# Recurrent branch of a hybrid block: turning the values, making the states and adding up the squares at other places

## The chip, the cores and the metric

The kernel runs on one core of a Trainium2 chip. The metric is the device time of one execution in microseconds (us). The engines are named as in the profile: PE (TensorE matmul), PEld (its weight loads), DVE (VectorE), ACT (ScalarE), POOL (GpSimd), SP (the queue that issues most transfers).

## The reference, cut to what matters

One encoder layer on 512 tokens of 1024 channels: a mixer of two branches (a gated linear recurrence, HGRN2, and a long convolution, Hyena), then a retrieval layer over 16384 experts (PEER). The change lies in the recurrence, which has 8 heads with 128 keys and 128 values, and runs over the tokens in both directions.

```python
def hgrn2_chunk_scan(q, k, logf, v):
    """S_t = diag(f_t) S_{t-1} + k_t v_t^T, o_t = S_t^T q_t, chunkwise."""
    ...
    def step(state, inp):
        qb, kb, fb, vb = inp
        b = jnp.cumsum(fb, axis=2)
        inter = jnp.einsum('nhtk,nhkv->nhtv', qb * jnp.exp(b), state)
        ...
        scores = jnp.einsum('nhtk,nhsk,nhtsk->nhts', qb, kb, decay)
        intra = jnp.einsum('nhts,nhsv->nhtv', scores, vb)
        new_state = (jnp.exp(b_last[:, :, 0, :, None]) * state
                     + jnp.einsum('nhsk,nhsv->nhkv', kb * jnp.exp(b_last - b), vb))
        return new_state, inter + intra
...
    o = o2[:B] + rev(o2[B:])
    o = rmsnorm(o, hgrn_norm_g).reshape(B, L, HGRN_WIDTH)
    y_a = jnp.einsum('blc,cd->bld', (o * jax.nn.silu(og.astype(f32))).astype(xn.dtype), w_branch_a)
```

The norm needs, for each token and head, the sum of the squares of 128 outputs. The queries, the two forget gates, the values and the output gate of each head are products of the normed input with 128 columns of the input weights.

## The kernel before, in words

Channels lie on the 128 partitions, the 512 tokens along the free dimension. The recurrence takes chunks of 128 tokens (4 of them), its scores are made from seven levels of decays (L692 is the line of their small matmuls, `quarters`), and states are carried over three chunk edges in each direction.

**Projection blocks.** A product with 128 columns of weights (`proj`, `product`) is 24 matmuls: weights and inputs are each split into a rounded upper part and a rounded rest (`split`: a cast on ACT, L94, and a subtraction on DVE, L95), and `mm3` adds up three of the four products, 16 matmuls (L103, L104) and then 8 (L106), all with fp32r operands. The result stands in one of three PSUM banks (`ps_mm`). The matmuls inside the recurrence have fp32 operands that are not rounded; a matmul with fp32 operands is shown as two instructions. They write to `ps_x`, five banks.

**One head.** Head `hd` runs `scores(hd)`, a generator that yields an estimate of its cost at each step, woven with `beside(hd, work)`, which supplies projection blocks for later heads: every 6.0 (6.4 for the last head) of cost spent, one more step of `beside` is emitted. Its four steps are a query block and an output gate block for head `hd + 1`, and two forget blocks for head `hd + 2` (or blocks of branch gates, where there are no more heads). The values block of the next head comes last. In the order of the code:

- `scores`: cumulated log forgets `Z`, decayed keys `KE` and queries `QE`, the transposes of the keys (L733) and their copies `KT` on ACT (L735). Then the decays: group (6, 0, 1, 2) of the levels, each a difference on DVE (L787, L788), an exponential on ACT (L790) and products on DVE (L769, L770), then their scores (L692); then `sigmoids(hd + 1)`; then group (3, 4, 5) with its scores. The exponentials of the second group are issued behind the sigmoids, and the sigmoids behind the last exponential of the first group and behind the inverse root (`rsqrt`, L125) of `normed(hd - 1)`.
- `beside`, step 0: the query block, then `outputs(hd - 1)` (L835, L837, L839 into `po`, and the squares `o2` on ACT, L841), then `transposed(hd)`, which turns the values `vT` (L654) and copies them to `vh` on ACT (L656).
- step 1: `normed(hd - 1)`, which adds up the squares over the partitions with a matmul by a 128x128 tile of ones (L847), takes the inverse root on ACT (L124, L125) and finishes the head on DVE (L850, L851); then the second block.
- `states`, called from `scores` after the first decays: six matmuls with `KT` and `vh` (L745), and the running states `S` on DVE (L752, L754).

The tiles come from pools with one (`w1`) or two (`w2`) buffers. All engine queues are ordered at compile time by a scheduler, which goes by the order in the code and by its own estimate of when the inputs of an instruction are there: an instruction that it takes to be late is put behind later ones of its engine. The order on the chip is then fixed.

## Time and profile before

| | |
|---|---|
| median of 3 runs | 2024.74 us (2024.29 to 2025.56) |
| profiled execution | 2028.34 us |
| its span in the trace | 2026.4 us |
| granted TensorE clock | 0.999 |
| busy: PE, PEld, DVE, ACT, POOL | 99%, 87%, 82%, 49%, 27% |
| the recurrence's stretch | about 370 to 668 us |

Start with busy times and the granted clock over the span, then the chain of work that ended last, then the waits of the recurrence. [...]

### The profile page before, as it was taken

How to read it: one execution, taken by the hardware profiler on the slowest of the kernel's cores; microseconds unless marked ns; L12 is line 12 of the kernel's file. 1: busy time of each engine (PE TensorE's matmuls, PEld its weight loads, DVE VectorE, ACT ScalarE, POOL GpSimd, SP SyncE). 2: the span in 40 equal slices, each digit the busy share in tenths (PEclk: the TensorE clock that was granted, in tenths of full speed). 3: DMA queues.
4: the chain of work that ended last, by engine and by line, in shares of the span. 5: the costliest groups of instructions: out<-in, count | busy, mean ns of one | idle time of the engine just before them, and what ended most of it. 6: DMA issues, size and time to landing. Idle time of an engine off the chain costs nothing.

```text
span 2026.4 us, 32597 instructions
## 1 busy us (share of the span) xinstructions
PE 2005.6 (99%) x12553; PEld 1772.0 (87%) x12553; DVE 1660.1 (82%) x3016; ACT 984.6 (49%) x1473; POOL 548.9 (27%) x331
## 2 busy tenths in 40 slices
PE   8999999999999999999999999999999999999998
PEld 6788888888888898889999998888888888888887
DVE  6788863889987637979999968878887899888885
ACT  6555443777785624436767643333333333333333
POOL 0000000000000000000000037676766677666660
PEclk9999999999999999999999999999999999999999
DMA  5212113222222434224767998988988898999884
GB/s 192 89 53 68 63 60 106 84 74 74 74 74 75 146 125 149 97 78 165 227 202 232 287 338 317 337 309 318 364 314 314 338 365 329 357 343 333 328 296 162
DMA packets 160410, 418.09 MB, mean 206 GB/s; under 512 B 12890, under 2 KB 66012, under 8 KB 160126
## 3 DMA queue, kind: packets, MB, share of 16 engines
q1 hardware_dynamic: 115180, 263.58, 37.0%
q0 software_dynamic: 36864, 134.23, 17.9%
q10 hardware_dynamic: 8210, 18.19, 2.6%
q8 instruction: 99, 1.62, 0.3%
q14 instruction: 57, 0.47, 0.1%
HBM read 377.94 MB, written 38.01 MB: 205 GB/s over the span
## 4 chain that ended last, share of the span: by engine, by line
PE 91%; DVE 3%; issue 2%; DMA 2%; POOL 1%; ACT 1%; DVEq 0%; ACTq 0%; POOLq 0%
PE ps_mm L103 11%; PE ps_mm L104 11%; PE ps_mm L106 10%; PE ps_a L104 8%; PE ps_a L103 8%; PE ps_a L106 8%; PE acc L1136 7%; PE acc L1135 7%; PE acc L1134 7%; PE ps_g L1421 4%; DMA grow<-in_u,gidx 2%; PE ps_x L103 1%; PE ps_x L106 1%; PE ps_x L104 1%; PE ps_x L692 1%
## 5 line engine op out<-in xcount | busy, mean ns | idle before, releaser
L103 PE MATMUL ps_a<-pxh,uh 128*128 128x384 f32 x1024 | 346.8, 339 | 0.4 <-ACT gact L986 0.3
L104 PE MATMUL ps_a<-pxl,uh 128*128 128x384 f32 x1024 | 343.9, 336 | 0.0
L95 POOL TENSOR_TENSOR ul<-uraw,uh 128x1024 fp32r<-128x1024 f32 x70 | 184.5, 2636 | 585.1 <-PE ps_a L106 433.9
L1135 PE MATMUL acc<-vl,gh 128*128 128x512 f32 x768 | 300.0, 391 | 1.6 <-DVE vl L95 1.5
L1134 PE MATMUL acc<-vh,gh 128*128 128x512 f32 x768 | 299.4, 390 | 0.0
L1136 PE MATMUL acc<-vh,gl 128*128 128x512 f32 x768 | 299.3, 390 | 0.0
L94 ACT CAST vh<-vraw 128x1024 fp32r<-128x1024 f32 x128 | 134.5, 1052 | 311.7 <-DMA vraw<-in_v 187.5
L103 PE MATMUL ps_mm<-xh,whi 128*128 128x512 f32 (+1 forms) x656 | 256.7, 393 | 0.4 <-ACT gt L265 0.4
L104 PE MATMUL ps_mm<-xl,whi 128*128 128x512 f32 (+1 forms) x656 | 254.2, 389 | 0.0
L1077 DVE SCALAR_TENSOR_TENSOR grow<-grow,xg 128x1024 f32<-128x1024 f32 x128 | 190.9, 1510 | 48.8 <-DMA grow<-in_u,gidx 48.5
L1089 DVE SCALAR_TENSOR_TENSOR xg<-grow,gw,xg 128x1024 f32<-128x1024 f32 x127 | 195.6, 1540 | 27.6 <-DMA grow<-in_v,gidx 26.0
L957 POOL IOTA iota<- 128x512 bf16 x1 | 1.2, 1189 | 759.4 <-PE ps_mm L106 759.4
L1048 POOL DMA_INDIRECT grow<-in_u,gidx x128 | 192.9, 1507 | 43.8 <-issue 24.4
L106 PE MATMUL ps_a<-pxh,ul 128*128 128x384 f32 x1024 | 198.3, 334 | 0.0
L103 PEld LDWEIGHTS ps_a<-pxh,uh 128*128 128x128 f32 x1024 | 192.4, 188 | 4.2 <-ACT gact L986 1.1
L104 PEld LDWEIGHTS ps_a<-pxl,uh 128*128 128x128 f32 x1024 | 192.7, 188 | 3.4
L95 DVE TENSOR_TENSOR vl<-vraw,vh 128x1024 fp32r<-128x1024 f32 x128 | 184.6, 1443 | 3.2 <-ACT vh L94 3.2
L95 DVE TENSOR_TENSOR wlo<-wraw,whi 128x1024 fp32r<-128x1024 f32 x112 | 136.5, 1220 | 60.6 <-ACT whi L94 32.6
L94 ACT CAST uh<-uraw 128x1024 fp32r<-128x1024 f32 x128 | 134.5, 1050 | 99.7 <-PE ps_a L104 76.6
L1048 POOL DMA_INDIRECT grow<-in_v,gidx x128 | 170.1, 1329 | 35.4 <-issue 20.8
L106 PEld LDWEIGHTS ps_a<-pxh,ul 128*128 128x128 f32 x1024 | 179.3, 188 | 0.0
L94 ACT CAST whi<-wraw 128x1024 fp32r<-128x1024 f32 x112 | 117.4, 1049 | 124.8 <-PE ps_mm L104 116.1
(420 smaller groups left out, 4000.2 us busy)
## 6 DMA issues: line engine op xcount, KB each, us to landing
uraw<-in_uT SPq DMA_DIRECT2D x128, 512.0 KB, 6.2
vraw<-in_v SPq DMA_DIRECT2D x128, 512.0 KB, 5.9
wraw<-in_w_in SPq DMA_DIRECT2D x80, 512.0 KB, 3.3
Gd<-Gs SPq DMA_DIRECT2D x12, 2048.0 KB, 9.6
gt<-Gd SPq DMA_DIRECT2D x32, 768.0 KB, 7.4
kept<-gact ACTq DMA_DIRECT2D x22, 384.0 KB, 2.5
gkept<-kept SPq DMA_DIRECT2D x22, 384.0 KB, 6.0
wraw<-in_w_q SPq DMA_DIRECT2D x16, 512.0 KB, 4.2
```

What stands on the lines that cost most here:

```text
L94: nc.scalar.copy(hi, src)
L95: return (eng or nc.vector).tensor_sub(lo, src, hi).ins
L103: nc.tensor.matmul(out, ah, bh, start=(i == 0), stop=False)
L104: nc.tensor.matmul(out, *((al, bh) if late else (ah, bl)), start=False, stop=False)
L106: nc.tensor.matmul(out, *((ah, bl) if late else (al, bh)), start=False, stop=(stop and i == n - 1))
L1048: nc.gpsimd.indirect_dma_start(out=t, out_offset=None, in_=tab, in_offset=bass.IndirectOffsetOnAxis(ap=gidx[:, j : j + 1], axis=0))
L1077: nc.vector.scalar_tensor_tensor(t, t, 1.0, xg, op0=ALU.mult, op1=ALU.mult, accum_out=gdot[h][:, i : i + 1])
L1089: nc.vector.scalar_tensor_tensor(gacc, t, gw[h][:, i : i + 1], gacc, op0=ALU.mult, op1=ALU.add)
L1134: nc.tensor.matmul(acc[k][c], gh[:, ts_], vh[:, ds_], start=(r == 0), stop=False)
L1135: nc.tensor.matmul(acc[k][c], gh[:, ts_], vl[:, ds_], start=False, stop=False)
L1136: nc.tensor.matmul(acc[k][c], gl[:, ts_], vh[:, ds_], start=False, stop=(r == NK - 1))
L1421: nc.tensor.matmul(pg[:, q * P : q * P + P], own[:, q], rows[:, q], start=True, stop=True)
```

## The change

- The values of a head are turned right behind its keys, in `scores`, instead of behind the outputs of the head before. Their copies `vh` have two buffers now.
- `states(hd)` is called in step 0 of `beside`, right behind `outputs(hd - 1)`, a block earlier.
- The squares `o2` are split into rounded halves `o2h` and `o2l` (a cast on ACT and a subtraction on DVE), and added up by two fp32r matmuls with a rounded tile of ones (`unit`) instead of one with fp32 operands.
- `normed(hd - 1)` is emitted inside the second block of `beside`, between its first 16 matmuls and its last 8, through a hook in `mm3`. The last head's comes behind a block, as before.
- `raw` (the forget gates' input) and `sct` (scores) have one buffer instead of two; `o2l` shares the slot of `vT`.

```diff
-def mm3(nc, out, terms, stop=True, late=0):
+def mm3(nc, out, terms, stop=True, late=0, between=None):
...
+    if between is not None:
+        between()
     for i, ((ah, al), (bh, bl)) in enumerate(terms):
         nc.tensor.matmul(out, *((ah, bl) if late else (al, bh)), start=False, stop=(stop and i == n - 1))
...
-    mm3(C.nc, ps, [((hi[:, k], lo[:, k]), (xh[:, k], xl[:, k])) for k in range(KB)])
+    between, C.between = C.between, None
+    mm3(C.nc, ps, [((hi[:, k], lo[:, k]), (xh[:, k], xl[:, k])) for k in range(KB)], between=between)
...
+    unit = cp.tile([P, P], F32R, name="unit")
+    nc.vector.memset(unit.bitcast(F32), 1.0)
...
-        raw = w2.tile([P, 2, L], F32, name="raw")
+        raw = w1.tile([P, 2, L], F32, name="raw")
...
-        vh = w1.tile([P, TB, P], F32, name="vh")
+        vh = w2.tile([P, TB, P], F32, name="vh")
...
-        sct = w2.tile([P, 4, 2, HALF], F32, name="sct")
+        sct = w1.tile([P, 4, 2, HALF], F32, name="sct")
...
             KTs.append(KT)
-        yield 6.0
+        transposed(hd)
...
+        after[hd] = states
+        yield 6.0
...
                 yield 3.1
-                if li == 0:
-                    states()
...
         nc.scalar.activation(o2, po, AF.Square)
-        st[hd] += [po, o2]
+        oh = w1.tile([P, L], F32R, name="o2h")
+        ol = w1.tile([P, L], F32R, name="o2l", tag="vT")
+        split(nc, oh, ol, o2)
+        st[hd] += [po, oh, ol]
...
-        nc.tensor.matmul(pm, C.ones, o2, start=True, stop=True)
+        nc.tensor.matmul(pm, unit, oh, start=True, stop=False)
+        nc.tensor.matmul(pm, unit, ol, start=False, stop=True)
...
             if i == 1 and hd:
-                normed(hd - 1)
+                C.between = lambda: normed(hd - 1)
             c = next(work)
             if i == 0:
                 if hd:
                     outputs(hd - 1)
-                transposed(hd)
+                after[hd]()
             yield c
```

## The prediction

> **What bounds the kernel now.** First the page: busy times, the slices' granted clock, the chain by engine.

> ```profile
> PE 2005.6 (99%) x12553; PEld 1772.0 (87%) x12553; DVE 1660.1 (82%) x3016; ACT 984.6 (49%) x1473; POOL 548.9 (27%) x331
> ...
> PEclk9999999999999999999999999999999999999999
> ...
> PE 91%; DVE 3%; issue 2%; DMA 2%; POOL 1%; ACT 1%; DVEq 0%; ACTq 0%; POOLq 0%
> ```

> TensorE is hardly ever idle, its clock is full throughout, and it carries 91% of the chain. So a microsecond of TensorE work or waiting that goes is a microsecond of time, if nothing new makes TensorE wait. A busy sum alone wouldn't say that, since matmul ends are modelled; the chain, which counts starts, does. Second, what one head (the fourth, index 3) looks like, in the stretches view (us; then PE, PEld, DVE, ACT, POOL busy):

> ```profile
> 440.00:476.00 36.00, 35.98 (x420) 29.67 (x418) 31.95 (x56) 27.55 (x42) 0.00 (x0) 1.00 0.22 74
> ```

> VectorE is busy 31.95 of 36 us here: second in line, 4 us from being the bound. Third, the chain in order of time (start, length, what), first two undisturbed projection blocks, then that head:

> ```profile
> 346.96 1.81 PE ps_mm L106 x8
> 352.40 1.81 PE ps_mm L106 x8
> ...
> 439.79 0.66 PE ps_x L733 x6
> 444.09 1.82 PE ps_mm L106 x8
> 448.14 0.44 PE ps_x L654 x4
> 448.83 1.12 PE ps_x L847 x2
> 453.38 1.82 PE ps_mm L106 x8
> 455.20 1.34 PE ps_x L745 x12
> 460.20 1.81 PE ps_mm L106 x8
> 462.01 1.73 PE ps_x L692 x114
> 467.59 1.81 PE ps_mm L106 x8
> 469.40 1.00 PE ps_x L692 x79
> 476.09 0.66 PE ps_x L733 x6
> ...
> 661.98 0.86 PE ps_x L847 x2
> ```

> A block of 24 rounded matmuls takes 352.40 − 346.96 = 5.44 us, 0.227 each. A head is 476.09 − 439.79 = 36.30 us: five blocks, and between them the full-precision groups: keys turned (L733), outputs (from 444.09 + 1.82 = 445.91 to 448.14: 2.23), values turned (L654), states (L745), and two of scores (L692). The sums of squares (L847) lie inside the second query block. Fourth, the waits of this stage (waited for, us in all, times, longest):

> ```profile
> PEld ps_x L847 <- ACT o L841: 2.0, 6, 0.3
> PEld ps_x L745 <- ACT vh L656: 2.1, 1, 2.1
> DVE hrs L850 <- ACT hrs L125: 12.9, 7, 2.7
> DVE KQ L678 <- ACT so L674: 11.1, 6, 1.9
> ```

> TensorE waits for ScalarE's squares by 0.33 us in six heads, and once, in the last head, 2.1 us for the turned values.

> **The change, part by part.**

> *Squares as two rounded products inside a block.* The block that now holds L847 runs from 448.14 + 0.44 = 448.58 to 455.20: 6.62 us against 5.44, so L847 costs 1.18, of which 0.33 is the wait. At a block's edge it costs 0.86 (661.98), which agrees with 1.18 − 0.33. Two rounded products of 512 columns cost 2 × 0.227 = 0.45. Six heads gain 1.18 − 0.45 = 0.73 each, 4.4 us; the last two sums of squares gain 0.86 − 0.45 = 0.41 each, 0.8 us.
> The wait of 0.33 can go only if the squares' rounded halves are there in time. On ScalarE and VectorE (start, length):

> ```profile
> 448.18 0.60 ACT L841 ACTIVATE o<-ps_x 128x512 f32<-128x512 f32 x1 [0.70 <-PE ps_x L837]
> 448.67 0.58 ACT L656 COPY vh<-ps_x 128x512 f32<-128x512 f32 x1
> 450.00 0.69 ACT L124 ACTIVATE hrs<-ps_x,epsc 128x512 f32<-128x512 f32 x1 [0.74 <-PE ps_x L847]
> ```
> ```profile
> 448.94 0.68 DVE L787 TENSOR_TENSOR Dt<-Z 128x512 f32<-128x512 f32 x1
> 451.38 0.69 DVE L850 TENSOR_TENSOR hrs<-ps_x,hrs 128x512 f32<-128x512 f32 x1 [1.76 <-ACT hrs L125]
> ```

> The new cast takes ScalarE 0.58 (as L656, whose place it takes) and the subtraction VectorE 0.68 (as L787): ready about 448.78 + 0.58 + 0.68, at most 0.7 more behind L787, so 450.0 to 450.8. The products now stand 1.34 (states) and 16 × 0.227 = 3.63 behind the outputs' end at 448.14, at 453.1. More than 2 us of cover; if that is gone, normed() is late next. So I take no wait here. The subtraction adds 0.68 to VectorE's 31.95, in a head that shrinks to some 35.5: it fits, by 2.9. In the last head L841 starts late, which the next fence shows: 631.97 + 0.58 + 0.58 + 0.68 = 633.8 against products at about 629.9 + 4.97 = 634.9; that fits by 1 us.

> *Values turned behind the keys, two buffers for them.* The one long wait of this stage, in the last head:

> ```profile
> 631.03 0.39 PE L104 MATMUL ps_mm<-xl,whi 128*128 128x512 f32 x1
> 633.07 1.60 PE L745 MATMUL ps_x<-vh,KT 128*128 128x128 f32 x12 [1.66 <-ACT vh L656]
> ```
> ```profile
> 631.00 1.06 ACT L790 ACTIVATE Dt<-Dt 128x1024 f32<-128x1024 f32 x1 [1.15 <-DVE Dt L788]
> 631.97 0.58 ACT L841 ACTIVATE o<-ps_x 128x512 f32<-128x512 f32 x1
> 632.44 0.58 ACT L656 COPY vh<-ps_x 128x512 f32<-128x512 f32 x1
> ```

> The copy of the turned values is queued behind a decay exponential that waits for VectorE. Turned a block earlier, they are copied before that; the 2.1 us go. What is late next there is the squares (above, 1 us to spare). In all heads the four transposes move from behind the outputs to behind L733: same count, no gain. But they need vT, which ScalarE copies only here:

> ```profile
> 441.37 1.05 ACT L790 ACTIVATE Dt<-Dt 128x1024 f32<-128x1024 f32 x1
> 442.33 0.56 ACT L647 COPY vT<-ps_mm 128x512 f32<-128x512 f32 x1
> ```

> L733 ends at 440.45, vT at 442.89: 2.4 us late, if ScalarE's order stays. The queues are ordered at compile time, by estimated readiness: L847 starts 0.25 us into a block that the code emits behind it. So I expect the transposes some matmuls into the block that follows. If the estimate is right this costs nothing; at worst 2.4 us a head.

> *States behind the outputs.* Six matmuls move one block ahead; their price, 1.34, is that of outputs (0.223 each), so only the return to rounded matmuls is saved: a block behind L745 takes 460.20 + 1.81 − (455.20 + 1.34) = 5.47 instead of 5.44, 0.03 in seven heads, 0.2 us. Their keys are copied behind L733, a block ahead, and the state updates on VectorE come earlier, into its idle time. No wait taken.

> *normed() later.* It moves from 0.69 us behind the outputs' end (448.83) to 4.97: 4.3 later. Queued behind it on ScalarE are sigmoids of the next head, then the last three decay exponentials of this one; on VectorE the products of these. The ends of that chain:

> ```profile
> 457.90 1.25 ACT L677 ACTIVATE lf<-sg,lbs,omlb 128x1024 f32<-128x1024 f32 x1
> 464.57 1.07 ACT L790 ACTIVATE Dt<-Dt 128x1024 f32<-128x1024 f32 x1 [0.39 <-DVE Dt L788]
> ```
> ```profile
> 467.25 0.68 DVE L770 TENSOR_TENSOR Dt<-KQ,Dt 128x512 f32<-128x512 f32 x1
> ```

> It ends at 467.93 and the second L692 starts at 469.40: 1.5 us of cover for a delay of 4.3. Without a move, L692 waits 2.8 us a head; moved 12 or so matmuls into the values block, it waits for nothing. Lower bound 0, upper 2.8; the nearest rows are the places at which a small group was put into a block, with waits of 0.33 six times and 2.1 once, so 0.33.

> *Single buffers, shared slots.*

> ```profile
> 453.63 1.04 ACT L672 ACTIVATE KQ<-raw 128x1024 f32<-128x1024 f32 x1
> ```
> ```profile
> 455.19 0.75 DVE L678 SCALAR_TENSOR_TENSOR KQ<-ps_mm,omlb,so 128x512 f32<-128x512 f32 x1 [1.85 <-ACT so L674]
> ```

> raw is last read by sigmoids at 454.67, 4.3 us later at 459.0, and next written after the first forget block (460.20 + 1.81 = 462.01, 1.3 us sooner when states and squares are out of its way: 460.7): 1.7 us to spare. The second forget block's bank of ps_mm is given up by L678 at 455.94 + 4.3 = 460.2, before the first L692 is over. sct, o2h, o2l (in the slot of vT): each reader is done before the next writer's input exists. No DMA, SP or POOL instruction moves.

> *Sum.* Gains 4.4 + 0.8 + 2.1 + 0.2 = 7.5. Against it the new early readers (L654, L733, L692, one lateness per head, since a wait that TensorE has had moves all later ones back): seven heads × 0.33 = 2.3. Net −5.2. The profiled execution took 2028.34 us (span 2026.4 and 1.9 around it), 3.6 above the median of 2024.74. It gives 2023.1, and on the median 2019.5.

> **Rivals.** *A. No new wait:* all 7.5 us, 2017.2. For it: the block edges where L733 and L692 stand now show no wait worth a row. It is the good end of my forecast.

> *B. The waits eat the gain.* 0.5 to 1.65 us a head for turned values or scores put in by an estimate that is early: 3.5 to 11.6 us against 7.5, so 2020.7 to 2028.8, no measurable change. For it: every group that was put inside a block shows a wait, never the opposite. Against: six of them are only 0.33.

> *C. The later normed() becomes the loop's bound: slower.* Sigmoids and decays stay queued behind it. Chain from L847's end (449.95) to L770's end: 18.0. TensorE from the second L692 to the next products, if L692 stays where it is: 1.00 + 5.69 (values block) + 0.66 + 0.44 + 5.46 + 2.23 + 1.34 + 3.63 + 0.45 = 20.9. Together 38.9, against 35.5 that TensorE needs for a head: 3.4 us a head, six heads, 20 us against 7.5, so 2037. It decides from 2.0 us a head on, that is if L692 is moved by fewer than six matmuls and nothing in the chain gets shorter. Against: of the 18.0, some is now TensorE's own (the exponential at 464.57 waits for a buffer that the first L692 frees), and that L692 will come 5 us sooner relative to normed().
> [...]

> **How the numbers follow.** This kernel's runs lie within 1.3 us, and about 0.2% (4 us) can be told from no change. My forecast, including A (0.15): 0.56, its own range 2016.5 to 2020.7. B: 0.26. C: 0.18, half of it beyond 2029. Low end: A with the larger price of a return to rounded matmuls (0.09 instead of 0.03 in seven heads) and the spread of runs: 2016. High end: where B ends, 2028.8. Faster needs less than 0.5 us of new wait a head: 0.56; same 0.26; slower 0.18.

> **What would show it.** Right: the sums of squares are 16 rounded matmuls (two a head) without a wait before them; the wait of 2.1 us for vh is gone; heads repeat at 35.5 to 36.0 us instead of 36.3; the rest of the program is only shifted. Wrong: TensorE waiting for vh or vT, for Dt or KE inside blocks by a us or more a head (B, C); heads of 37 us with L692 waiting for Dt (C); a block with the squares that isn't 5.44 + 0.45 (my first term); or another order of work after 670 us.

## The result, and the profile after

The changed kernel is slower: 2041.2 us median of 4 runs (2038.52 to 2042.37) against 2025.03 us before (2024.29 to 2025.56), ratio 1.0078, 95% interval 1.0063 to 1.0093. The forecast was 2019.5 us, range 2016.0 to 2028.8; rival C, at 2037, had a chance of 0.18.

The page of the changed kernel, the same lines as before (busy times, the chain by engine):

```profile
PE 2005.2 (98%) x12553; PEld 1773.3 (87%) x12553; DVE 1658.3 (81%) x3025; ACT 991.2 (49%) x1481; POOL 552.5 (27%) x331
...
PE 89%; ACT 6%; DVE 3%; issue 1%; DMA 0%; DVEq 0%; ACTq 0%
```

This page shows 2005.2 us of PE work, 0.4 less than before, in a span that is 13 us longer, and 6% of the chain now lies on ScalarE. Where the time went is seen from first and last starts of two groups, before and then after: the keys' transposes (first head, last head), and the first product behind the recurrence.

```profile
L733 PE MATMUL ps_x<-ident,KE x48: 271/272/273, 370.4 to 622.1; 128*128 128x128 f32 x48
L103 PE MATMUL ps_mm<-yah,whi x64: 393/394/399, 668.2 to 710.6; 128*128 128x512 f32 x64
```
```profile
L739 PE MATMUL ps_x<-ident,KE x48: 271/273/328, 370.3 to 640.1; 128*128 128x128 f32 x48
L103 PE MATMUL ps_mm<-yah,whi x64: 393/394/399, 684.0 to 726.5; 128*128 128x512 f32 x64
```

From the first keys to the last: 251.7 us before, 269.8 after, 18.1 more. From the last keys to the next stage: 46.1 before, 43.9 after, 2.2 less. So the last head gained, as forecast, and the loop over the heads lost. The recurrence to its next stage grew by 15.8 us (668.2 to 684.0), as much as the medians (16.2); the span grew by 13.2 alone, since the profiled execution of before, at 2028.3 us, lay 3.3 above its median, and that of the changed kernel, at 2042.4, 1.2 above. Most of what made it long lies behind the recurrence: from the next stage's first product to the end of the span it took 1358.2 us (2026.4 − 668.2), the changed kernel 1355.6.

The waits of the recurrence after the change (lines moved: L739 keys, L660 values, L698 scores, L126/L127 inverse root, L856/L857 squares):

```profile
DVE hrs L860 <- ACT hrs L127: 21.0, 7, 3.5
PEld ps_x L660 <- ACT vT L653: 8.2, 8, 2.6
PEld ps_x L739 <- DVE KE L729: 7.4, 6, 1.3
PE ps_x L698 <- DVE Dt L778: 4.6, 5, 0.9
```

The waits for the squares and for vh, the turned values' copies, are gone. In their place TensorE waits for turned values, for decayed keys and for decays. One head on TensorE, the small groups alone:

```profile
437.70 0.76 PE L698 MATMUL ps_x<-Dt 128*32 128x32 f32 x64
439.38 0.46 PE L698 MATMUL ps_x<-Dt 128*32 128x32 f32 x32 [0.91 <-DVE Dt L778]
...
446.37 0.87 PE L739 MATMUL ps_x<-ident,KE 128*128 128x128 f32 x6 [0.87 <-DVE KE L729]
447.66 0.66 PE L660 MATMUL ps_x<-ident,vT 128*128 128x128 f32 x4 [0.42 <-ACT vT L653]
...
460.88 0.39 PE L856 MATMUL ps_x<-o2h,unit 128*128 128x512 f32 x1
461.11 0.39 PE L857 MATMUL ps_x<-o2l,unit 128*128 128x512 f32 x1
...
476.12 0.76 PE L698 MATMUL ps_x<-Dt 128*32 128x32 f32 x64
477.81 0.46 PE L698 MATMUL ps_x<-Dt 128*32 128x32 f32 x32 [0.93 <-DVE Dt L778]
```

From the second L698 row to the last, 439.38 to 477.81, a head is 38.4 us (36.3 before). The products of the squares stand where they were meant to, between two halves of a block, without a wait. But the last third of the scores, which would have needed to move some ten matmuls into the next block, stands right behind its block and waits for its decays; the keys wait for VectorE, and the values for ScalarE. Three waits are on record in each head; which of them counts can't be read off, since one that TensorE has had shortens the next. ScalarE in the same stretch shows the queue behind the sums of squares:

```profile
461.08 1.05 ACT L94 CAST whi<-wraw 128x1024 fp32r<-128x1024 f32 x1 [3.75 <-PE ps_mm L104]
462.04 0.68 ACT L126 ACTIVATE hrs<-ps_x,epsc 128x512 f32<-128x512 f32 x1
...
464.70 1.06 ACT L677 ACTIVATE sg<-raw 128x1024 f32<-128x1024 f32 x1
...
469.47 1.25 ACT L683 ACTIVATE lf<-sg,lbs,omlb 128x1024 f32<-128x1024 f32 x1
...
475.29 1.05 ACT L798 ACTIVATE Dt<-Dt 128x1024 f32<-128x1024 f32 x1
```

ScalarE stands idle for 3.75 us, until TensorE is through the first 16 matmuls of the block and the squares behind them; then it runs inverse root, sigmoids and the last decays back to back; the decays end at 476.3, and VectorE's product behind them is what the scores at 477.81 wait for.

### The profile page after: what moved, and what is told of

Same layout as the page of the kernel before. It is cut to its first block, busy times and chain, and to the rows that moved or that the text cites. A ratio compares the mean times of both kernels' runs of the same rounds, so it can differ in the third digit from the quotient of the medians.

```text
span 2039.6 us, 32593 instructions
## 1 busy us (share of the span) xinstructions
PE 2005.2 (98%) x12553; PEld 1773.3 (87%) x12553; DVE 1658.3 (81%) x3025; ACT 991.2 (49%) x1481; POOL 552.5 (27%) x331
## 4 chain that ended last, share of the span: by engine, by line
PE 89%; ACT 6%; DVE 3%; issue 1%; DMA 0%; DVEq 0%; ACTq 0%
PE ps_mm L103 9%; PE ps_mm L104 9%; PE ps_a L104 9%; PE ps_a L103 9%; PE ps_a L108 9%; PE acc L1144 9%; PE acc L1145 9%; PE acc L1146 9%; PE ps_mm L108 8%; PE ps_g L1431 4%; PE ps_x L103 1%; PE ps_x L108 1%; PE ps_x L104 1%; ACT whi L94 1%; ACT Dt L798 1%; PE ps_s L1276 1%
## 5 line engine op out<-in xcount | busy, mean ns | idle before, releaser
L95 POOL TENSOR_TENSOR ul<-uraw,uh 128x1024 fp32r<-128x1024 f32 x70 | 188.8, 2697 | 582.4 <-PE ps_a L108 435.6
L104 PE MATMUL ps_a<-pxl,uh 128*128 128x384 f32 x1024 | 343.9, 336 | 0.0
L104 PE MATMUL ps_mm<-xl,whi 128*128 128x512 f32 (+1 forms) x656 | 252.8, 387 | 0.0
L1087 DVE SCALAR_TENSOR_TENSOR grow<-grow,xg 128x1024 f32<-128x1024 f32 x128 | 184.4, 1460 | 50.5 <-DMA grow<-in_u,gidx 48.9
L95 DVE TENSOR_TENSOR vl<-vraw,vh 128x1024 fp32r<-128x1024 f32 x128 | 195.9, 1531 | 4.6 <-ACT vh L94 4.6
L104 PEld LDWEIGHTS ps_a<-pxl,uh 128*128 128x128 f32 x1024 | 192.7, 188 | 3.5
L1058 POOL DMA_INDIRECT grow<-in_v,gidx x128 | 169.5, 1324 | 35.5 <-issue 22.4
```

What stands on the lines that cost most here:

```text
L95: return (eng or nc.vector).tensor_sub(lo, src, hi).ins
L104: nc.tensor.matmul(out, *((al, bh) if late else (ah, bl)), start=False, stop=False)
L1058: nc.gpsimd.indirect_dma_start(out=t, out_offset=None, in_=tab, in_offset=bass.IndirectOffsetOnAxis(ap=gidx[:, j : j + 1], axis=0))
L1087: nc.vector.scalar_tensor_tensor(t, t, 1.0, xg, op0=ALU.mult, op1=ALU.mult, accum_out=gdot[h][:, i : i + 1])
```

## The experiments

Each batch ran on one chip, with the kernel before beside it. All differences are under 2%; faster or slower is said where the interval of the ratio leaves out 1. "Head" is the distance from one head's keys (in the changed kernel and e1_edge: values) to the next's, near 440 us.

| run | what | us | ratio (95%) | head, us |
|---|---|---|---|---|
| before | | 2025.2 to 2025.5 | 1 | 36.3 |
| changed | | 2041.2 | 1.0063 to 1.0093 | 38.4 |
| e1_edge | changed, no hook | 2035.7 | 1.0033 to 1.0061 | 37.6 |
| e2_hook | before + hook | 2023.8 | 0.9980 to 0.9999 | 36.0 |
| e3_squares | before + rounded squares | 2025.2 | 0.9988 to 1.0007 | 36.2 |
| e4_moves | before + both moves | 2045.1 | 1.0071 to 1.0103 | 39.9 |
| v_only | before + values behind keys | 2038.6 | 1.0048 to 1.0079 | 38.1 |
| s_only | before + states behind outputs | 2025.5 | 0.9993 to 1.0011 | 36.3 |
| x_e4 | both moves, values block earlier | 2026.0 | 0.9994 to 1.0012 | 36.0 |
| n2_hooksq | before + hook + rounded squares | 2024.2 | 0.9983 to 1.0001 | 36.5 |
| x_after | changed, values block earlier | 2035.1 | 1.0032 to 1.0063 | 37.8 |
| x_e1 | changed, no hook, values block earlier | 2031.7 | 1.0021 to 1.0045 | 37.2 |
| z2_late_only | changed, squares out of the loop | 2035.0 | 1.0030 to 1.0061 | 37.6 |
| z1_both | changed, both cures | 2020.1 | 0.9965 to 0.9984 | 35.6 |
| y4_late3 | before + squares out of the loop | 2020.7 | 0.9968 to 0.9986 | 35.6 |
| y6_turn | y4_late3, `so` in two tiles, values turned ahead of outputs | 2021.6 | 0.9978 to 0.9996 | 35.7 |

**Taking the change apart.** The first theory was rival C. It was tried by undoing the hook, and by doing each part alone.

```diff
 e1_edge (on the changed kernel)
-                C.between = lambda: normed(hd - 1)
+                normed(hd - 1)
 e2_hook (on the kernel before): only `between` in mm3 and product, and
-                normed(hd - 1)
+                C.between = lambda: normed(hd - 1)
 e3_squares (on the kernel before): only unit, o2h, o2l and two products
 e4_moves (on the kernel before): only the places of transposed() and states()
```

> The changed kernel with one thing undone: normed(hd - 1) is emitted ahead of the second block again, not between its 16th and 17th matmul; squares stay rounded, values and states stay where the change put them. Theory 1 (the late sums of squares: one head's loop runs from them over the inverse root, the sigmoids, the last decays, the scores, the next keys and values back to them, and is now longer than TensorE's work): the waits of TensorE for Dt, KE and vT inside a head (0.9 + 0.9 + 0.4 us) go, a head repeats at 35.5 to 36.0 us, time 2017 to 2021 us. Theory 2 (the turned values behind the keys, or the single buffers, make the waits by themselves): heads stay near 38.4 us, time 2037 to 2041 us.

> The kernel before with only the hook: normed(hd - 1), still with the one full-precision matmul, is emitted after the 16th matmul of the second block; values, states and buffers as before. Theory 1: the sums of squares come 3.4 us later, against 1.5 us of cover, so heads 1 to 6 grow by up to 2 us less the 0.33 us of the wait that goes: 2027 to 2037 us. Theory 2: no new wait, the 0.33 us of six heads go: 2022 to 2025 us.

> The kernel before with only the rounded squares (two products with the tile unit, emitted where the one matmul was, ahead of the second block); sct has one buffer and o2l shares the slot of vT, to make room. Theory 1: the sums come about 1.3 us later (a cast and a subtraction more), inside the 1.5 us of cover; eight times 0.41 us of TensorE go: 2021 to 2023 us. Rival (the subtraction on a VectorE that is 88% busy, or the longer way, costs as much as it saves): 2024 to 2028 us.

> The kernel before with only the moves: values turned behind the keys (two buffers for them, one for sct to make room), states behind the outputs; squares with one full-precision matmul ahead of the second block. Theory 1: the sums come 0.9 us later, inside the 1.5 us of cover; the 2.1 us of the last head go: 2021 to 2024 us. Theory 2: TensorE waits for vT and KE in each head as in the changed kernel: 2030 us or more.

The hook alone made the kernel no slower, and theory 1 as the whole cause fell. Without the hook 10 of the 16 us stayed, between what theory 1 gave (2017 to 2021 us) and what theory 2 gave (2037 to 2041). The moves alone cost 20, more than the change. In the kernel with the moves alone, TensorE and then ScalarE:

```profile
445.10 0.82 PE L733 MATMUL ps_x<-ident,KE 128*128 128x128 f32 x6
...
448.43 0.66 PE L654 MATMUL ps_x<-ident,vT 128*128 128x128 f32 x4 [2.05 <-ACT vT L647]
```
```profile
445.05 0.82 ACT L825 COPY sct<-near 64x256 f32<-64x256 f32 x2 [2.07 <-DVE near L818]
445.89 1.04 ACT L94 CAST whi<-wraw 128x1024 fp32r<-128x1024 f32 x1
446.85 1.05 ACT L792 ACTIVATE Dt<-Dt 128x1024 f32<-128x1024 f32 x1
447.81 0.57 ACT L647 COPY vT<-ps_mm 128x512 f32<-128x512 f32 x1
```

The values block ends as the keys are turned, at 445.1. The copy of it stands fourth in this part of ScalarE's queue, behind copies that wait for VectorE, a cast and an exponential. TensorE's order has the transposes two matmuls into the block that follows: it stands still for 2.05 us. The rounded squares ahead of the block (e3) put their own wait where the 0.33 us had been, and so gave nothing:

```profile
PEld ps_x L853 <- DVE o2l L95: 2.6, 6, 0.6
...
PEld ps_x L852 <- ACT o2h L94: 1.7, 6, 0.3
```

**Which move, and is it vT.** Theory 3 and its rival were tried by each move alone, and by making vT earlier with both moves in place.

```diff
 v_only (on the kernel before): transposed(hd) behind L735, states() where it was
 s_only (on the kernel before), step 0 of beside
+                transposed(hd)
                 if hd:
                     outputs(hd - 1)
-                transposed(hd)
+                after[hd]()
 x_e4 (on e4_moves) and x_after, x_e1 (below)
-            work, per = chain(queried(hd + 1), forgets(hd + 2) ...
+            work, per = chain(queried(hd + 1), valued(hd + 1), forgets(hd + 2) ...
...
-            values(hd + 1)
+            next(work)
```

> The kernel before with the values turned behind the keys and nothing else (vh has two buffers, sct one to make room; states where they were, squares as before). Theory 3 (the transposes behind the keys need vT, whose block ends just when they stand, and ScalarE copies it 2 us later than the fixed order allows for; each head TensorE stands 2 us, and where such a wait fills a window of the clock, the clock is halved for 3.4 us on top): waits of about 2 us for vT in every head, 2035 to 2046 us. Rival theory 4 (it is the states a block earlier that hold up the head): 2021 to 2026 us.

> The kernel before with the states behind the outputs, and the values turned ahead of the outputs, in the same group, not behind the keys (vh two buffers, sct one; squares with one full-precision matmul ahead of the second block). Theory 3: no wait for vT, which is there a block earlier; the 2.1 us of the last head may go too: 2021 to 2026 us. Theory 4: 2030 us or more.

> The kernel with only the moves (values behind the keys, states behind the outputs) and the block that makes the next head's values one place earlier: third of the five blocks of a head, the second forget block takes its place as the last. So vT is there a block before the keys. Theory 3: the wait of 2 us for vT goes from every head and the clock stays full: 2020 to 2026 us, 20 us under the same moves without this. Theory 4: 2035 us or more, as without it.

> The kernel before with the two rounded products and the hook, without any move of values or states (sct one buffer, o2l in the slot of vT). If the sums of squares inside the block cost only their two products there: six heads of 36.30 us lose 0.73 us each, the last two sums 0.41 each: 2019 to 2021.5 us. Theory 1 in its weaker form (late sums cost something as soon as they are later by more than the hook alone made them): 2023 to 2026 us.

```profile
PE ps_x L654 <- ACT vT L647: 11.4, 7, 1.7
```

That is the kernel with the values behind the keys alone: seven waits of up to 1.7 us, 13 us of time. Theory 3's halved clock was read from the kernel with the moves alone, where 3.42 us at 0.50 came behind a wait of 2.05 us that took 2.00 of the 3.41 us before them (last section); here it did not come, and the clock over the span is 1.000. States a block earlier, with the values turned just ahead of the outputs, cost nothing and gave nothing. With the values block one place earlier the moves cost nothing either (2026.0 against 2045.1): theory 3 held. In the kernel with hook and rounded squares, the expected 4 to 6 us did not come. Its chain, and a wait of it:

```profile
439.12 0.88 PE ps_x L739 x6
...
475.59 0.87 PE ps_x L739 x6
```
```profile
PEld ps_x L739 <- DVE KE L729: 5.4, 6, 1.0
```

A head takes 36.47 us, and the keys wait for VectorE: with the squares later and TensorE's own work shorter, the loop over the squares does bind. Theory 1 was back, as a second cause.

**Two causes.** The full change with the values block earlier; the same without the hook; and, on the kernel before, the sums of squares taken out of the loop.

```diff
 y4_late3 (on n2_hooksq)
-            if i == 1 and hd:
+            if i == 2 and hd:
                 C.between = lambda: normed(hd - 1)
...
-                with tc.issue_after(e.ins), tc.issue_after(rsqrt[-1] if hd else e.ins):
+                with tc.issue_after(e.ins):
...
-        so = w2.tile([P, 2, L], F32, name="so")
+        so = w2.tile([P, 2, L], F32, name="so", bufs=3)
-        raw = w2.tile([P, 2, L], F32, name="raw")
+        raw = w1.tile([P, 2, L], F32, name="raw")
```

The third buffer is needed because sigmoids(hd + 1) otherwise waits for normed(hd - 1) through the slot of so.

> The changed kernel, all of it, with the block for the next head's values one place earlier (third of five; the second forget block is last). Theory 3 (vT, made by the last block ahead of the keys, is what the changed kernel waits for): its wait for vT goes and with it most of the 16 us: 2021 to 2028 us, the upper part if the loop over the late sums of squares still holds keys up by some tenths of a us a head. Theory 1 alone (late sums): 2035 us or more, as the change.

> As the kernel with the values block earlier, but the sums of squares ahead of the second block, not inside it (no hook). Theory 3: no wait for vT; a wait for the rounded squares at the block's edge instead, about 0.7 us a head: 2020 to 2026 us. If the hook costs something by itself through the loop, this is faster than the one with the hook; if not, it is slower by about 0.7 us in six heads.

> The kernel before with rounded squares and the hook one block later, in the first forget block, and with the sigmoids of the next head no longer behind the inverse root of the head before (so has three buffers for that, raw and sct one). It takes the sums of squares out of the loop squares - inverse root - sigmoids - decays - keys. Theory 5 (this loop is what keeps the rounded squares and the hook from showing: a head cannot be shorter than 36.0 to 36.5 us with it, while TensorE needs 35.6): heads of 35.6 us, no wait for KE, 2019 to 2022 us. If another limit (VectorE's 32.6 us a head with its waits) holds it: 2023 to 2026 us.

In the full change with vT early, only 6 of the 16 us went: theory 3 missed by 7 us, and 2035.1 us lies at the edge of what theory 1 alone gave. Its heads, without a wait for vT:

```profile
443.15 0.87 PE L739 MATMUL ps_x<-ident,KE 128*128 128x128 f32 x6 [0.86 <-DVE KE L729]
443.86 0.60 PE L660 MATMUL ps_x<-ident,vT 128*128 128x128 f32 x4
...
473.93 0.46 PE L698 MATMUL ps_x<-Dt 128*32 128x32 f32 x32 [0.93 <-DVE Dt L778]
...
480.91 0.88 PE L739 MATMUL ps_x<-ident,KE 128*128 128x128 f32 x6 [0.86 <-DVE KE L729]
```

37.76 us a head, with waits of 0.93 us for decays and 0.86 for keys, both behind the late sums. Without the hook (x_e1) it is faster by 3.4 us, so the hook does cost through this loop, but at 2031.7 us it isn't free either (2020 to 2026 were expected); there the products stand at the block's edge, right behind the states, and their halves are late:

```profile
452.56 0.50 PE L857 MATMUL ps_x<-o2l,unit 128*128 128x512 f32 x1 [1.05 <-DVE o2l L95]
```

With the sums out of the loop, the kernel before gains 4.6 of the 5.2 us that the rounded squares and the hook were priced at (4.4 + 0.8), its one long wait being the last head's:

```profile
PEld ps_x L751 <- ACT vh L662: 2.1, 1, 2.1
```

**Both cures on the full change.** The same edit as y4_late3 on x_after; there so is two tiles, so that only the gate's has three buffers.

> The changed kernel with both suspects taken away: the values block one place earlier, and the sums of squares out of the loop (hook in the third block, sigmoids not behind the inverse root; the query's and the gate's sigmoids lie in tiles of their own, so that the gate's can have three buffers). Theory 6 (two causes, each of which hides behind the other: vT behind the keys is late by itself, and the later squares hold up the sigmoids, the decays and the keys of the next head by themselves): with both gone heads are 35.5 us and the last head's wait for vh is gone too: 2016 to 2021 us. If something else in the change costs (states a block earlier, the single buffers): 2024 us or more.

> The changed kernel with only the second suspect taken away: sums of squares out of the loop as in the kernel with both, the values block where the change has it, ahead of the keys. Theory 6: the wait for vT stays or grows, waits for KE and Dt go: 2028 to 2038 us. If the late squares were all that costs: under 2024 us.

> The kernel before with rounded squares in the third block, out of the loop, as in the best run so far (2020.7 us), and the values turned just ahead of the outputs instead of behind them (vh two buffers), states where they were. If the last head's 2.1 us wait for vh goes with it: 2017.5 to 2020 us. If the copy stays behind the same decay exponential on ScalarE: 2020 to 2022 us.

| the changed kernel, us | squares in the loop | out of the loop |
|---|---|---|
| values block ahead of the keys | 2041.2 | 2035.0 |
| values block one place earlier | 2035.1 | 2020.1 |

Each cure alone gives 6 us, both give 21. A head takes 35.6 us with neither cause, 37.8 with the late squares alone, 37.6 with the late vT alone and 38.4 with both: little more than the longer of the two, and far from their sum. The 0.6 us more has a likely place: in the changed kernel's chain the copy of vT (447.04 us on ScalarE) comes behind the exponentials of keys and queries, which the late squares hold up. Of the 6 us that an earlier values block gives, some 4 come from one head, the second (41.7 us from keys to keys, 37.7 in x_after), where a wait of 2.13 us for vT was followed by a stretch at half clock (0.50 for 3.41 us, last section). "Out of the loop" is a bundle, a later hook, sigmoids that no longer wait for the inverse root and the buffers for it; its parts were not tried one by one. The kernel with only the squares cured shows the other cause by itself; the kernel with both shows neither behind its first head, and keys 35.60 us apart:

```profile
447.78 0.66 PE L660 MATMUL ps_x<-ident,vT 128*128 128x128 f32 x4 [1.80 <-ACT vT L653]
```
```profile
441.17 0.82 PE L739 MATMUL ps_x<-ident,KE 128*128 128x128 f32 x6
441.83 0.60 PE L660 MATMUL ps_x<-ident,vT 128*128 128x128 f32 x4
...
476.77 0.82 PE L739 MATMUL ps_x<-ident,KE 128*128 128x128 f32 x6
```

With 2020.1 us this is as fast as y4_late3 (2020.7), and both beat the kernel before and the changed one. Single buffers and the states' place are in it, and cost nothing that shows. It has lost the last head's wait for vh, but in its first head TensorE waits 1.25 us for vT. y6_turn lost the wait for vh too, 43.3 us from the last keys to the next stage against 45.3 in y4_late3, but is no faster; 2017.5 to 2020 us were expected. Its trace shows what took at least part of the 2 us back:

```profile
571.33 0.38 PE L698 MATMUL ps_x<-Dt 128*32 128x64 f32 x10 [1.82 <-issue]
```

TensorE stands still for 1.82 us ahead of the last scores of one head, and nothing in the profile releases it ("issue"). The changed kernel has such a pause of 1.91 us at the same scores, v_only one of 2.4, y4_late3 one of 0.3. What makes it stays open.

## Why the prediction was wrong, step by step

- *The squares' price: right.* The hook alone took the 0.33 us wait from each head (36.30 to 35.98 in e2), and rounded products with no loop in the way took the rest: 36.30 to 35.65 in y4_late3, to 35.60 in z1, 0.65 to 0.70 against 0.73 forecast. That the halves would be ready was right too: no wait at L856 or L857 in the changed kernel.
- *The last head's 2.1 us: right.* From the last keys to the next stage 2.2 us went.
- *States behind the outputs: right*, no cost (s_only, x_e4).
- *The term that failed* is that of the new early readers, 7 × 0.33 = 2.3 us. The loop over the heads grew by 18.1 us, although the squares' 4.4 us were to come off it; so in place of 2.3 us stand some 22 (18.1 + 4.4), most of them from the next two steps.
- *Values behind the keys: this step failed.* The bounds were 0 and 2.4 us a head, the value taken 0.33, from rows of other groups that had been put inside a block. Measured: 1.7 to 2.1 us in single heads, 13 us in all alone. The row that mattered was the one beside the bound: vT copied 2.4 us behind the keys, with three instructions ahead of it in ScalarE's queue. I let the compile-time order close that gap by "some matmuls"; it moved the transposes by two, 0.45 us, in the kernels with this move, and in the changed kernel from the third head on by none. What the groups in the rows of before had in common was that their input came late by little, so their waits said nothing about one that is late by 2.4.
- *normed() later: this step failed as well.* Cover 1.5 us, delay 4.3, and again 0.33 taken on the hope that the scores would move 12 matmuls. They did not move: two thirds ran at the old place and the rest waited 0.93 us there. The price was 37.8 − 35.6 = 2.2 us a head (x_after), where C had 3.4; C said that some of its chain would shorten, and the difference fits that, without a run that shows which part.
- *"One lateness per head": right but for 0.6 us, and it is why the parts don't add.* 38.4 us with both causes, 37.8 and 37.6 with one.
- C's mechanism, the later normed(), was there, and alone it gave 2035.1 us (x_after) against C's 2037. That 2037 also came near the changed kernel's 2041 is in part luck, since the late vT, which C left out, is in the 2041 as well. The forecast had both in its bounds, and took the low end of both.

C took what is queued behind a late instruction to wait with it. With the moves alone one copy did: that of vT started at 447.81 us, fourth in line on ScalarE, though the block that it copies had ended at about 445.1, 2.7 us before.

## What to carry to other kernels

When a step is moved next to the work that makes its input, look up in the consumer's trace how late that input is now and what stands ahead of it in the copying engine's queue; if the gap is longer than the work in between, take the gap less that work as the price (here 2.4 − 0.45, about 2.0 us; measured 1.7 to 2.1) and not the mean of other waits. On an engine that is full, a gain in its own work shows only as long as no loop over the other engines takes as long: with the hook and the rounded squares a loop of 36.5 us took over, and they gave 1 us until the sums were taken out of it, 4.6 then. If curing one of two suspected causes gives little, cure both before dropping either.

## What the runs showed of the hardware

```profile
446.42:449.83 3.41, 1.41 (x8) 1.25 (x9) 3.41 (x6) 3.41 (x6) 0.00 (x0) 1.00 0.00 0
449.83:453.25 3.42, 3.42 (x9) 2.67 (x8) 3.42 (x6) 1.79 (x3) 0.00 (x0) 0.50 0.42 153
...
483.96:487.38 3.42, 2.31 (x14) 1.63 (x12) 3.42 (x7) 2.41 (x4) 0.00 (x0) 1.00 0.08 30
487.38:490.79 3.41, 2.48 (x13) 2.13 (x14) 3.41 (x6) 3.08 (x6) 0.00 (x0) 1.00 0.18 42
```
```profile
450.27 0.63 PE L104 MATMUL ps_mm<-xl,whi 128*128 128x512 f32 x1
450.69 0.63 PE L103 MATMUL ps_mm<-xh,whi 128*128 128x512 f32 x1
```

The wait of 2.05 us that ended at 448.43 lies almost whole in the first of these stretches. In the next 3.42 us the clock is at 0.50, and matmuls start 0.42 us apart instead of 0.227. The same came behind four of the waits of that kernel (2.04 to 2.12 us, so its moves alone cost more than the change: 39.9 us in that head, 38.3 in one without), and behind one in the changed kernel (2.13 us), in e1_edge (2.1), in z2_late_only and in x_e1 (2.12).

The length of the wait doesn't decide alone. The four slow stretches of that kernel begin at 408.88, 449.83, 565.89 and 644.39 us, which is 12, 34 and 23 times 3.413 us apart: they lie on one grid of windows of that length. The wait of 2.04 us that ended at 488.31 is cut by an edge of this grid, at 487.38, into 1.11 and 0.93 us, and the clock stayed at 1.00. It did so in the changed kernel behind the pause of 1.91 us that ended at 587.60, which the grid of its own slow stretch cuts at 586.35 into 0.66 and 1.25, and behind the pause of 2.4 us in v_only. In the recurrence of the changed kernel, cut along that grid, the window with the wait of 2.13 us is the only one with half clock behind it:

```profile
405.45:408.86 3.41, 1.28 (x9) 0.80 (x8) 3.41 (x6) 3.38 (x7) 0.00 (x0) 1.00 0.00 0
408.86:412.28 3.42, 3.42 (x10) 2.65 (x9) 3.42 (x6) 2.45 (x3) 0.00 (x0) 0.50 0.47 152
```

The other windows there hold up to 1.28 us of idle TensorE, and the clock behind them is 1.00. In the kernel before, 1.66 us idle between 631.00 and 634.41 left it at 1.00 too. So 2.00 us idle in one window (3.41 − 1.41, above) had half clock behind it and 1.66 had not; what lies in between isn't shown. The ends of matmuls are modelled, so these sums are rough. The page's slices show 9, that is 90% or more, throughout; only a window of a few microseconds shows the loss.
